# Strassen's algorithm for three weight products of a two-block transformer

## The chip, the cores and the metric

The kernel runs on one core of a Trainium2 chip. The metric is the device time in microseconds (us). The engines are TensorE (PE, the products), VectorE (DVE), ScalarE (ACT), GpSimd (POOL) and SyncE (SP, which issues the transfers from memory).

## The reference

512 tokens of 1024 features pass through two blocks of two layers each, in float32. Every layer is a mixer and then a feed-forward part, each with a normed input `h` of shape [512, 1024]:

```python
# first block, layers l = 0, 1
x = x + rms_norm(mixed @ w_out[l], attn_post_g[l])
h = rms_norm(x, ffn_pre_g[l])
y = (jax.nn.silu(h @ w_gate[l]) * (h @ w_up[l])) @ w_down[l]    # 1024 -> 2816 -> 1024
x = x + rms_norm(y, ffn_post_g[l])
# second block, layers 0 (stick-breaking attention) and 1 (a gated recurrence)
a = jax.nn.relu(h @ w1)                                         # 1024 -> 4096 -> 1024
x = x + (a * a) @ w2
```

The mixers of the first block are differential and forgetting attention. Most of the arithmetic is in the products with weights.

## The kernel before

**Numbers.** PE takes float32 in a rounded form (float32r). Each operand is kept as a high and a low part, and `mm3` (line 623) makes every product out of three: high x high, high x low, low x high. `split_into` (line 525) makes the parts: a copy (`cp`, line 313, on ACT or DVE) and a subtraction on DVE (`tt`, line 286).

**Order.** The program is first written down as a list of operations (`Program`, line 150). `schedule` (line 365) then plays it through with a cost for each operation: an engine that is free takes what is ready and due first, where `due_times` (line 335) counts back from a PE that runs without a gap in program order. A tile gets its slot when its first writer is placed; a slot is taken ahead of program order only if the rest could still run. The order found is fixed for each engine. SBUF is cut into slots by `KINDS`: 61 of 528 words ("S") for weight parts, hidden tiles and attention tiles, three raw chunks of 4.1 KB, one normed input in two parts (`xh`, `xl`), two gain rows. PSUM has four banks "A" and four "B".

**Weights.** `Stream` (line 529) loads chunks of 1024 columns (512 KB), two ahead of use, and splits each in two halves of 512.

**The feed-forward part.** `ffn` (line 1155) goes over 22 column tiles of w_gate and w_up in passes of 8, 8 and 6, `mlp` (line 1177) over 32 of w1 in four passes of 8. In a pass `proj_fm` (line 630) makes [128 features, 512 tokens] in a bank: 8 tiles of the 1024 inputs x 3 products, a weight tile of 128x128 stationary and 512 tokens moving. Then silu and the product with up (or relu and square), and the split into two parts. `proj_out` (line 667) multiplies the pass's hidden tiles by w_down or w2: hidden tiles stationary, 512 columns of weights moving.

**The entry.** The output projection ahead of a feed-forward part goes token tile by token tile (four of 128 tokens): `finish` norms the tile (`norm_tile`, line 732), and its `place` turns it on PE, four 128x128 transposes for each half of the features, and writes the parts (`cp` on ACT, the subtraction on DVE). The place of a tile comes a tile later in program order. The first four column tiles of a stage are done with `cut`: all products of tokens 0 to 255 first, then those of 256 to 511.

## Time and profile before

| what | value |
|---|---|
| median of 3 runs | 2561.39 us (2561.36 to 2562.69) |
| profiled execution, span | 2558.8 us |
| PE busy | 2524.3 us (99%) |
| DVE busy | 1591.4 us (62%) |
| ACT busy | 940.7 us (37%) |
| first feed-forward stage, with its down products | 275 to 632 us |
| second | 902 to 1258 us |
| first MLP | 1549 to 1908 us |
| second MLP | 2198 to 2559 us |

The times of the page are of one profiled execution, 2.6 us shorter than the median of the runs. An engine's busy time counts the time that its instructions last; PE's products overlap, so that the distance from one start to the next is their real price. A row of the time line gives its start, how long the group lasted, the engine, the line of the code, the operation, its tiles (output, then inputs) and shapes, and how many there are; a bracket at its end is the engine's idle time ahead of it.

### The profile page before, as it was taken

The page shows a single profiled execution, that of the slowest core. Times are in us where ns is not written, and L with a number is a line of the kernel's source. Part 1 is how long each engine was busy: PE and PEld are TensorE (multiplying, and loading weights), DVE is VectorE, ACT ScalarE, POOL GpSimd, SP SyncE. Part 2 cuts the span into 40 slices and gives each one's busy share as a digit, 9 for nine tenths or more (in the row PEclk, how much of TensorE's full clock was granted, in tenths as well). Part 3 has the DMA queues.
Part 4 walks back from the last instruction along what each step waited for, and adds up shares of the span by engine and source line. Part 5 has one row for each costly group of instructions (what it writes and reads, how often), then busy time and mean ns, then how long its engine had stood idle before and what let it go on. Part 6 is the DMA issues. An engine that isn't in the chain of part 4 may idle for free.

```text
span 2558.8 us, 36752 instructions
## 1 busy us (share of the span) xinstructions
PE 2524.3 (99%) x14060; PEld 2103.5 (82%) x14060; DVE 1591.4 (62%) x3742; ACT 940.7 (37%) x2170; POOL 57.2 (2%) x78
## 2 busy tenths in 40 slices
PE   7999999999999999999999999999999999999999
PEld 7987888888997788888898768888888887888887
DVE  8867843345886773334698887444557778744442
ACT  5656422222565532222356564222233333422210
POOL 0000000000000000000000000000000111000000
PEclk9999999999999999999999999999999999999999
DMA  6221433231322152323131114332314111342220
GB/s 204 67 83 50 137 102 99 74 116 42 109 83 67 50 181 76 97 75 115 50 100 58 42 50 149 116 99 67 106 37 129 59 59 50 118 129 76 88 77 33
DMA packets 63856, 225.12 MB, mean 88 GB/s; under 512 B 7344, under 2 KB 7984, under 8 KB 63680
## 3 DMA queue, kind: packets, MB, share of 16 engines
q1 hardware_dynamic: 63680, 222.77, 27.6%
q8 instruction: 111, 1.82, 0.3%
q14 instruction: 65, 0.53, 0.1%
HBM read 220.61 MB, written 2.13 MB: 87 GB/s over the span
## 4 chain that ended last, share of the span: by engine, by line
PE 95%; DVE 4%; issue 1%; ACT 0%; DMA 0%; SPq 0%; DVEq 0%; ACTq 0%
PE A L235 73%; PE B L235 18%; PE B L245 4%; DVE S L289 1%; DVE S L310 1%; DVE sm L304 1%; ACT S L256 0%; DVE x L304 0%; DMA gb<-in_rows_dram 0%; DVE S L317 0%; ACT xh L256 0%; DVE sm L298 0%; DVE xl L289 0%; DVE sm L297 0%; DVE S L318 0%
## 5 line engine op out<-in xcount | busy, mean ns | idle before, releaser
L235 PE MATMUL A<-xh,S 128*128 128x512 f32 (+1 forms) x3328 | 984.6, 378 | 0.0
L289 DVE TENSOR_TENSOR S<-raw,S 128x512 fp32r<-128x512 f32 (+1 forms) x792 | 523.5, 690 | 341.8 <-PE A L235 204.6
L235 PEld LDWEIGHTS A<-xh,S 128*128 128x128 f32 x3328 | 604.8, 188 | 118.0 <-issue 0.7
L235 PE MATMUL A<-xl,S 128*128 128x512 f32 (+1 forms) x1664 | 629.6, 379 | 0.0
L256 ACT ACTIVATE S<-raw 128x512 fp32r<-128x512 f32 (+1 forms) x632 | 380.9, 630 | 657.4 <-PE A L235 383.3
L235 PE MATMUL A<-S,S 128*128 128x512 f32 (+1 forms) x2088 | 511.9, 394 | 0.0
L235 PE MATMUL B<-S,S 128*128 128x512 f32 (+12 forms) x2448 | 501.2, 369 | 0.7 <-DVE S L289 0.5
L235 PEld LDWEIGHTS B<-S,S 128*128 128x128 f32 (+2 forms) x2448 | 363.2, 179 | 112.4 <-issue 31.7
L235 PEld LDWEIGHTS A<-S,S 128*128 128x128 f32 x2088 | 384.8, 188 | 83.1 <-issue 0.5
L235 PE MATMUL A<-S,xh 128*128 128x256 f32 (+1 forms) x2048 | 377.2, 286 | 0.5 <-ACT xh L256 0.2
L235 PEld LDWEIGHTS A<-xl,S 128*128 128x128 f32 x1664 | 313.0, 188 | 61.4 <-issue 0.7
L256 ACT ACTIVATE S<-A 128x512 f32<-128x512 f32 (+3 forms) x238 | 140.6, 593 | 470.0 <-PE A L235 462.4
L235 PEld LDWEIGHTS A<-S,xh 128*128 128x128 f32 x2048 | 309.3, 189 | 3.0 <-ACT xh L256 0.8
L235 PE MATMUL A<-S,xl 128*128 128x256 f32 (+1 forms) x1024 | 268.2, 285 | 1.9 <-DVE xl L289 1.9
L256 ACT ACTIVATE S<-B 128x128 f32<-128x128 f32 (+7 forms) x560 | 163.7, 360 | 110.5 <-PE B L235 64.5
L235 PEld LDWEIGHTS A<-S,xl 128*128 128x128 f32 x1024 | 183.5, 189 | 3.0 <-DVE xl L289 2.2
L289 DVE TENSOR_TENSOR S<-S,S 128x512 fp32r<-128x512 f32 (+4 forms) x234 | 133.6, 584 | 70.2 <-PE A L235 51.7
L245 PE MATMUL B<-cst,S 128*128 128x128 f32 x872 | 135.8, 276 | 27.5 <-DVE sm L298 11.5
L245 PEld LDWEIGHTS B<-cst,S 128*128 128x128 f32 x872 | 103.5, 141 | 45.2 <-DVE sm L298 11.5
L317 DVE CAST S<-raw 128x512 fp32r<-128x512 f32 (+1 forms) x160 | 68.3, 430 | 68.7 <-PE A L235 45.1
L289 DVE TENSOR_TENSOR S<-A,S 128x512 f32<-128x512 f32 (+1 forms) x68 | 46.9, 689 | 96.2 <-PE A L235 95.6
L289 DVE TENSOR_TENSOR S<-S 128x512 f32<-128x512 f32 (+2 forms) x68 | 45.5, 669 | 97.4 <-ACT S L256 55.7
(116 smaller groups left out, 1327.2 us busy)
## 6 DMA issues: line engine op xcount, KB each, us to landing
raw<-in_mlp_dram SPq DMA_DIRECT2D x128, 512.0 KB, 3.6
raw<-in_w_gate_dram SPq DMA_DIRECT2D x44, 512.0 KB, 3.6
raw<-in_w_up_dram SPq DMA_DIRECT2D x44, 512.0 KB, 3.8
raw<-in_w_down_dram SPq DMA_DIRECT2D x44, 512.0 KB, 3.7
raw<-in_w_in_tm_dram SPq DMA_DIRECT2D x28, 512.0 KB, 3.8
raw<-in_sb_qkv_dram SPq DMA_DIRECT2D x24, 512.0 KB, 4.0
raw<-in_hg_fm_dram SPq DMA_DIRECT2D x24, 512.0 KB, 3.9
raw<-in_w_in_fm_dram SPq DMA_DIRECT2D x16, 512.0 KB, 4.2
```

The costliest lines, as they stand in the source:

```text
L235: self.nc.tensor.matmul(_ap(ps), _ap(l), _ap(r), start=start, stop=stop)
L245: o = self.op([("pe", 109.0, lambda: pe.transpose(_ap(ps), _ap(src), _ap(ident)))], [src, ident], [ps])
L256: return self.nc.scalar.activation(_ap(out), _ap(src), func, **kw)
L289: alts.append(("dve", self._dve_ns(out.n), lambda: self.nc.vector.tensor_tensor(_ap(out), _ap(a), _ap(b), op)))
L304: lambda: self.nc.vector.scalar_tensor_tensor(_ap(out), _ap(a), _ap(s), _ap(b), op0, op1))],
L310: lambda: getattr(self.nc.vector, name)(_ap(out), *[_ap(v) for v in a], **kw))],
L317: return self.nc.vector.tensor_copy(_ap(out), _ap(src))
```

## The change

One level of Strassen's algorithm (in Winograd's form) for h @ [w_gate | w_up] and h @ w1. The tokens are cut in two halves, the 1024 inputs in two, and a pair of 256-column blocks of weights is the other side; seven products of half-size blocks replace eight.

- `Forms` takes the place of the normed input: seven forms of the input's blocks (a11, a12, a22, s1 to s4), each in two parts of 4 KB. Token tiles 0 and 1 give a11 and a12. Tiles 2 and 3 give s1 to s4 and a22 by four sums on DVE, and five turned tiles.
- `sched_quad` loads the four blocks of weights, makes the four sums t1, t2, t3, t4 of them on DVE, and splits seven blocks.
- `proj_quad` makes the seven products, each 24 of 256 columns (two column tiles x 4 input tiles x 3), into three banks, and adds some products up in PSUM by going on in a bank whose value was read out. Five sums out of PSUM are left to DVE, and one copy to ACT.
- Weights of all products come in slots of 4 KB (31 of kind "W", which also hold the raw chunks, the input's parts or forms, gain rows, queries, values and transposed probabilities); 30 slots of 2 KB ("S") hold the rest. Splits are of 1024 elements. Loads run up to 5 and splits up to 3 products ahead in the seven-product units.
- The square of relu may go to ACT or DVE, before it was DVE or POOL. The `cut` of a stage's first tiles is gone.

```diff
 KINDS = {
-    "S": (61, "sbuf"), "mv": (1, "sbuf"), "xh": (1, "sbuf"), "xl": (1, "sbuf"), "raw": (3, "sbuf"), "gb": (2, "sbuf"),
-    "sm": (24, "sbuf"), "rot": (4, "sbuf"), "A": (4, "psum"), "B": (4, "psum"),
+    "W": (31, "sbuf"), "S": (30, "sbuf"), "sm": (16, "sbuf"), "rot": (2, "sbuf"), "A": (4, "psum"), "B": (4, "psum"),
 }
-SLAB = 528
+SLAB = {"W": 1024, "S": 512}
...
+        def split(self, v, n):
+            w = g.tile("W", (n,), F32R), g.tile("W", (n,), F32R)
+            split_into(v, w[0].all(), w[1].all())
             return w
...
+    def sched_quad(key, blocks):
...
+        def add(out, a, b):
+            if out not in v:
+                v[out] = g.tile("W", (1024,))
+            g.tt(v[out].all(), v[a].all(), v[b].all(), ALU.add)
+
+        def make(nm, *sums):
+            def run():
+                for t in sums:
+                    add(*t)
+                return ws.split(v[nm].all(), 1024)
+            return run
...
+        plan[key] = [
+            ws.add(load(0), make(0)),
+            ws.add(load(1, 3), chain(rename("t1", 0), make("t2", ("t1", 0, 1), ("t2", "t1", 3)))),
+            ws.add(none, make("t1")),
+            ws.add(none, chain(rename("t3", 1), make("t3", ("t3", 1, 3)))),
+            ws.add(load(2), make(2)),
+            ws.add(none, make(3)),
+            ws.add(none, chain(rename("t4", "t2"), make("t4", ("t4", "t2", 2)))),
+        ]
...
+    def proj_quad(key, forms):
...
+        ids = plan[key]
+        a, c, d = PSA(), PSA(), PSA()
+
+        def product(n, bank, f, first=False):
+            wh, wl = ws.get(ids[n], (L_LOOK, F_LOOK))
+            xh, xl = forms[f]
+            for u in range(2):
+                for k in range(4):
+                    sl = slice(k * 256 + u * P, k * 256 + u * P + P)
+                    dst = bank[:, u * 256:(u + 1) * 256]
+                    one = first and not u and not k
+                    g.mm(dst, wh[:, sl], xh[:, k, :], one, False, True)
+                    g.mm(dst, wh[:, sl], xl[:, k, :], False, False, True)
+                    g.mm(dst, wl[:, sl], xh[:, k, :], False, k == 3, True)
+
+        p1, u2, u3, c12, c21, c22 = [SL() for _ in range(6)]
+        product(0, a, "a11", True)
+        g.cp(p1.all(), a.all(), only="act")
+        product(1, c, "s2", True)
+        g.tt(u2.all(), c.all(), p1.all(), ALU.add)
+        product(2, d, "s1", True)
+        product(3, c, "s3")
+        g.tt(u3.all(), c.all(), p1.all(), ALU.add)
+        g.tt(c22.all(), d.all(), u3.all(), ALU.subtract)
+        product(4, a, "a12")
+        yield 0, 0, a.all()
+        yield 1, 1, c22.all()
+        product(5, d, "s4")
+        g.tt(c12.all(), d.all(), u2.all(), ALU.subtract)
+        yield 1, 0, c12.all()
+        product(6, c, "a22")
+        g.tt(c21.all(), c.all(), p1.all(), ALU.add)
+        yield 0, 1, c21.all()
...
+    class Forms:
...
+        def put(self, f, h, t):
+            w = self.xs[f]
+            put_parts(w[0][:, 0:4, tok(t % 2)], w[1][:, 0:4, tok(t % 2)], turned(h))
+
+        def finish(self, t, gain):
+            hs = norm_tile(t, gain)
+            if t >= 2:
+                (a11, a12), (a21, a22) = self.held.pop(t - 2), hs
+                s1, s2 = SL(), SL()
+                g.tt(s1.all(), a21.all(), a22.all(), ALU.subtract)
+                g.tt(s2.all(), s1.all(), a11.all(), ALU.subtract)
+                g.tt(a21.all(), a11.all(), a21.all(), ALU.subtract)
+                g.tt(a12.all(), a12.all(), s2.all(), ALU.add)
+
+            def place():
+                if self.xs is None:
+                    self.xs = new_forms()
+                if t < 2:
+                    self.put("a11", hs[0], t)
+                    self.put("a12", hs[1], t)
+                    self.held[t] = hs
+                else:
+                    for f, h in (("s2", s2), ("s1", s1), ("s3", a21), ("s4", a12), ("a22", a22)):
+                        self.put(f, h, t)
...
     def ffn(l, xs, pre, nxt):
         def up(lo, hi):
-            parts = []
+            blocks = []
             for j in range(lo, hi, 2):
...
+                for n, t, v in proj_quad(("gu", l, j), xs):
+                    if n == 0:
+                        gate[t] = SL()
+                        g.a(gate[t].all(), v, AF.Silu)
+                    else:
+                        out[t] = v
+                for t in range(2):
+                    g.tt(gate[t].all(), out[t], gate[t].all(), ALU.mult)
+                blocks.append([hidden(gate[t].all()) for t in range(2)])
```

## Rows read from the trace of the kernel before

**Rows 1.** Page, busy time of each engine with its share of the span.

```profile
PE 2524.3 (99%) x14060; PEld 2103.5 (82%) x14060; DVE 1591.4 (62%) x3742; ACT 940.7 (37%) x2170; POOL 57.2 (2%) x78
```

**Rows 2.** Waits of PE: total us, times, longest (ten rows).

```profile
PE B L245 <- DVE sm L298: 11.5, 1, 11.5
PE B L245 <- DVE S L317: 8.1, 6, 1.7
...
PE A L235 <- DVE xl L289: 1.9, 1, 1.9
...
PE A L235 <- DVE S L289: 0.2, 1, 0.2
```

**Rows 3.** Chain that ended last: shares, then pieces (start, us, what).

```profile
PE 95%; DVE 4%; issue 1%; ACT 0%; DMA 0%; SPq 0%; DVEq 0%; ACTq 0%
...
27.12 29.31 PE A L235 x248
...
365.54 22.21 PE B L235 x96
387.76 111.12 PE A L235 x480
...
2198.69 4.49 PE A L235 x38
```

**Rows 4.** Groups by line and form: count, busy us and mean ns, idle before.

```profile
L235 PE MATMUL A<-xh,S 128*128 128x512 f32 x2816 | 893.1, 396 | 0.0
L235 PEld LDWEIGHTS A<-xh,S 128*128 128x128 f32 x3328 | 604.8, 188 | 118.0 <-issue 0.7
L235 PE MATMUL A<-xl,S 128*128 128x512 f32 x1408 | 557.8, 397 | 0.0
...
L235 PE MATMUL A<-xh,S 128*128 128x256 f32 x512 | 92.1, 282 | 0.0
...
L235 PE MATMUL A<-xl,S 128*128 128x256 f32 x256 | 71.8, 280 | 0.0
```

**Rows 5.** Time line of PE at the entry of the first feed-forward stage.

```profile
266.83 7.74 PE L235 MATMUL A<-S,S 128*128 128x512 f32 x33
274.42 1.03 PE L245 MATMUL B<-cst,S 128*128 128x128 f32 x8
275.21 0.36 PE L235 MATMUL A<-xh,S 128*128 128x256 f32 x1
...
284.87 1.03 PE L245 MATMUL B<-cst,S 128*128 128x128 f32 x8
```

**Rows 6.** Time line of PE at the entry of the first MLP.

```profile
1548.16 1.04 PE L245 MATMUL B<-cst,S 128*128 128x128 f32 x8
...
1553.48 1.03 PE L245 MATMUL B<-cst,S 128*128 128x128 f32 x8
```

**Rows 7.** Rates of DVE and ACT: time line rows, then groups by form.

```profile
287.35 2.49 DVE L289 TENSOR_TENSOR S<-raw,S 128x512 fp32r<-128x512 f32 x4
...
1550.38 2.71 ACT L256 ACTIVATE S<-raw 128x512 fp32r<-128x512 f32 x5
...
L317 DVE CAST S<-raw 128x512 fp32r<-128x512 f32 x156 | 66.5, 430 | 65.6 <-PE A L235 45.1 <-DMA raw<-in_mlp_dram 5.2 <-PE B L235 4.9
...
L289 DVE TENSOR_TENSOR S<-S,S 128x511 f32<-128x511 f32 x16 | 10.3, 684 | 0.0
...
L289 DVE TENSOR_TENSOR S<-S,S 128x383 f32<-128x383 f32 x16 | 8.9, 554 | 0.9
```

**Rows 8.** Stretch: its length, busy of PE, PEld, DVE, ACT, POOL; clock, DMA, GB/s.

```profile
286.00:308.00 22.00, 22.00 (x151) 20.30 (x150) 18.75 (x34) 7.65 (x14) 0.00 (x0) 1.00 0.63 206
```

**Rows 9.** The start: stretch with its granted clock, then time line rows.

```profile
18.00:20.50 2.50, 2.35 (x13) 2.29 (x13) 2.50 (x14) 1.77 (x3) 0.00 (x0) 1.00 0.46 125
...
18.80 0.63 PE L235 MATMUL A<-S,xh 128*128 128x256 f32 x2
19.23 0.41 PE L235 MATMUL A<-S,xl 128*128 128x256 f32 x1
```

More of the change, by code (lines that the diff above doesn't have):

```diff
@@ L552, in ahead, with __init__ @@
-        def ahead(self, i):
-            while self.n < len(self.todo) and self.n <= i:
-                self.emit(self.n)
-                self.n += 1
-        def get(self, ids):
-            w = []
-            for i in ids:
-                self.ahead(i + self.look)
-                w += self.done.pop(i)
-            return w
-    ws = Stream(W_LOOK)
-    plan = {}
-    def sched(key, a, width=1024):
-        plan[key] = [ws.add(a[:, c:min(c + width, a.shape[-1])]) for c in range(0, a.shape[-1], width)]
+        def __init__(self):
+            self.todo, self.done = [], {}
+            self.loaded = self.made = 0
@@ new lines, in add, with ahead @@
+        def add(self, load, make):
+            self.todo.append((load, make))
+            return len(self.todo) - 1
+        def split(self, v, n):
+            w = g.tile("W", (n,), F32R), g.tile("W", (n,), F32R)
+            split_into(v, w[0].all(), w[1].all())
+            return w
+        def ahead(self, i, looks=(W_LOOK, W_LOOK)):
+            for what, look in ((0, looks[0]), (1, looks[1])):
+                at = self.made if what else self.loaded
+                while at < len(self.todo) and at <= i + look:
+                    if what:
+                        self.done[at] = self.todo[at][1]()
+                    else:
+                        self.todo[at][0]()
+                    at += 1
+                if what:
+                    self.made = at
+                else:
+                    self.loaded = at
@@ new lines, in get, with raw_load, sched @@
+        def get(self, i, looks=(W_LOOK, W_LOOK)):
+            self.ahead(i, looks)
+            return self.done.pop(i)
+    def raw_load(src):
+        n = src.shape[-1]
+        v = g.tile("W", (n,))
+        g.dma(v.all(), src, nbytes=P * n * 4)
+        return v
+    ws = Stream()
+    plan = {}
+    def sched(key, a, n):
+        k, per = a.shape[-1] // n, 1024 // n
+        ids = []
+        for c in range(0, k, per):
+            src, box = a[:, c * n:min(c + per, k) * n], []
+            ids.append(ws.add(lambda src=src, box=box: box.append(raw_load(src)),
+                              lambda box=box: ws.split(box[0].all(), box[0].dims[0])))
+        plan[key] = (ids, per, n, k)
@@ L651, in proj_tm, with x_part, proj_fm, tokens_by @@
+    def x_part(xs, k, sl):
+        return tuple(w[:, k % 2, sl] for w in xs[k // 2])
+    def proj_fm(key, xs):
+        part, ps = weights(key), PSA()
+        for k in range(KT):
+            mm3(ps.all(), part(k), x_part(xs, k, slice(0, S)), k == 0, k == KT - 1)
+        return ps
+    def tokens_by(ps, t, part, xs):
+        for k in range(KT):
+            mm3(ps, x_part(xs, k, tok(t)), part(k), k == 0, k == KT - 1)
     def proj_tm(key, xs):
-        slabs = ws.get(plan[key])
+        part = weights(key)
@@ L667, in proj_out @@
     def proj_out(key, parts, evac, finish=None, banks=(PSA, PSA)):
+        kn = plan[key + (0,)][3]
         if finish:
-            slabs, rest = [ws.get(plan[key + (c,)]) for c in range(2)], []
+            part, rest = [weights(key + (c,)) for c in range(2)], []
             for t in range(NT):
@@ L756, in norm_tile, with turned, put_parts @@
-        return place
+        return hs
+    def turned(h):
+        tr = PSB()
+        for k in range(4):
+            g.tr(tr[:, tok(k)], h[:, tok(k)], ident)
+        return tr.all().rearrange("p (k t) -> p k t", k=4)
+    def put_parts(dst, lo, src):
+        g.cp(dst, src, only="act")
+        g.tt(lo, src, dst.bitcast(F32), ALU.subtract)
     def END(t):
         return lambda: None
-    class Next:
+    class Plain:
         xs = None
-        def placing(self, place):
-            def run():
+        def finish(self, t, gain):
+            hs = norm_tile(t, gain)
+            def place():
@@ L931, in attn_pair @@
     def attn_pair(vtile, probs):
-        pts = [[SL() for _ in range(NT)] for _ in range(2)]
+        two = [g.tile("W", (2, S)) for _ in range(NT)]
+        pts = [[w[:, hh, :] for w in two] for hh in range(2)]
         ready = {}
```

287 lines of the change are left out of this document (152 added, 135 removed).

## The prediction

> **What bounds the kernel now.** I read the page's busy table first [rows 1]: TensorE (PE) is busy 99% of the 2558.8 us span, VectorE (DVE) 62%, ScalarE (ACT) 37%. A pipelined PE can look busy without being at its rate, so I then read the list of all that PE waited for [rows 2]: ten rows, 30.8 us in all, of which 13.4 us belong to the start (the first row and the xl row). Some 17 us are left in 2545 us. The chain that ended last says the same: PE holds 95% of it [rows 3], and in the feed-forward stages it is one unbroken run of products. So a microsecond of PE work that goes is a microsecond of span, until another engine or a wait is late.
>
> Two pitches carry the sum, both start to start. A product of 512 columns: 480 of them in 111.12 us, 96 in 22.21 us, so 231.4 ns [rows 3]. A product of 256 columns against a 128x128 stationary tile: 248 in 29.31 us in the projections, 38 in 4.49 us in the token-half group of an MLP, so 118.2 ns [rows 3]; the latter has the very operand form (weights stationary, 256 tokens moving) that the change uses everywhere. Half the columns cost 51%. A single weight load lasts 188 ns [rows 4], and loads and products overlap: neither pitch holds a whole one.
>
> **The products.** Take as a unit two gate and two up column tiles (FFN) or four w1 tiles (MLP): 38 units, 11 in each FFN and 8 in each MLP. The groups by form confirm the count: 2816+1408 products of 512 columns with x moving, less 960 of other projections, are 34 units of 96, and 512+256 of 256 columns are 4 units done by token halves (192 each) [rows 4]. A unit is 96 x 231.4 ns = 22.21 us now. Seven half-size products are 7 x 24 = 168 of 256 columns, 168 x 118.2 ns = 19.86 us. Gain 2.35 us x 38 = 89.5 us; the four halved units cost 192 x 118.2 = 22.69 us each now, 0.48 us more, so 1.9 us go too: **-91.4 us**.
>
> What could undo this is the weight load that comes with each product, 168 a unit in place of 96. In the token-half group a load and its product, on full 128-row tiles, take 118.2 ns together [rows 3, 4]. The Trainium skill, "TensorE: Matmul & The Clock Gate", section "The mechanism" (Part 3), says otherwise: that a weight load overlaps running products only where it goes to other rows of the array. By that rule a unit would take at least 168 x 188 ns = 31.6 us; the trace disagrees, and I take the row (the rule's case is rival d).
>
> **More transposes.** Token tiles 2 and 3 now turn five half-width forms each (20 transposes) instead of two (8): 24 more at each of four entries to a feed-forward stage. Eight go by in 0.79 us (274.42 to 275.21) [rows 5]: 96 x 0.099 = **+9.5 us**, on PE and not hidden.
>
> **The entry to each stage.** Now, when the last output product of token tile 3 ends, PE does the first unit on token tiles 0 and 1 while tile 3 is normed. At the first FFN that lasts from 275.21 to the transposes of tile 3 at 284.87, 10.5 us after the products ended at about 274.4; at an MLP, with one norm instead of two, from 1548.1 to 1553.48, 5.3 us [rows 5, 6]. The cover was up to 96 products, 11.3 us. After the change only the a11 product and, if its weights are ready, the a12 product need no token of tile 3: 24 x 0.1182 = 2.84 us each, with 2.0 us for the transposes of tile 2. The chain grows too: two DVE sums until s2 (2 x 0.60), three more low parts of tile 2 on the busy DVE (1.8), then transpose, ACT copy, low part (0.4 + 0.2 + 0.6 + 0.7) and hand-overs of some 0.4. That puts the s2 product at 10.5 + 5.3 = 15.8 us (FFN) or 5.3 + 5.3 = 10.6 us (MLP) after the last output product, against a cover of 4.8 to 7.7 us. Idle: 8.1 to 11.0 us at an FFN, 2.9 to 5.8 us at an MLP. Some of the chain is slack (two weight splits lie in it), so I take 8.5 and 4: 2 x 12.5 = **+25 us**, bounds 16 and 34.
>
> **DVE and ACT in the units.** This is where it can fail. A 512-element DVE add or subtract repeats every 0.60 us (four in 2.49 us) and lasts 1.02 ns per element more (511 against 383 elements: 684 and 554 ns) [rows 7], so one of 1024 is 0.60 + 0.53 = 1.13 us. A unit now needs 8 low parts of weights, 4.8 us. After: 7 low parts and 4 sums of 1024 (12.5 us), five sums out of PSUM (3.0), four more for the hidden tiles (2.4): 17.9 us per 19.86 us of PE, 90% of it. ACT: a 512 copy repeats every 0.52 us (five in 2.71) [rows 7], so one of 1024 takes 1.04 us at most: 7 x 1.04 + 0.5 + 2.1 = 9.9 us (FFN), 14.0 us (MLP, with squares). DVE just fits, and PE waits only where a bank is handed over late. The tightest: the a12 product (2.84 us) runs while DVE must form u3 and then c22 before the s4 product may add to bank d. That is 0.2 + 0.60 + 0.69 + 0.2 = 1.7 us, and up to 1.13 us more if a weight split has just begun: 2.83 us against 2.84. One split more between the two costs 1.1 us. I take 0.15 us per unit, **+6 us**; bounds 0 (nothing below: the product rate is measured) and 1.0 us per unit, 38 us. In the first 22 us of the first FFN DVE was already busy 18.75 us [rows 8], and PE had no idle there. The down products follow each few units at a third of that load, so a lag is caught up only as far as buffers allow.
>
> DMA carries the same weights: four loads of 512 KB per unit, some 106 GB/s, against 206 GB/s seen in that stretch [rows 8]. On SP's queue a load that waits for one of the 31 W slots holds up the gain rows and the weights behind it; the splits ahead wait for those. Stretches with 14 slots held by the seven forms are the place to look.
>
> **Everything else.** Attention and the recurrent mixer keep their products, with 4 KB and 2 KB slots (31 and 30) in place of 61 small ones and tiles of their own. A start split is 0.53 us longer per part. No row shows what the new partition costs; the nearest is the 17 us of PE waits left in the span [rows 2], which could vanish or double: -17 to +17, and I take **+4 us** since long splits get in the way of short chains.
>
> **Sum.** -91.4 + 9.5 + 25 + 6 + 4 = -46.9 us. The profiled span of 2558.8 us would be 2511.9; the median of the runs is 2.6 us above that span, so **2514.5 us**.
>
> **Rivals.** (a) The entries are well covered and DVE is in time: 16 for entries, 0 for hand-overs, -5 for the rest: 2561.4 - 91.4 + 9.5 + 16 - 5 = 2490.5 us. For it: the planner does work as soon as it is due. Chance 0.17.
>
> (b) PE loses its clock at the entries. At the start, after 11.5 us of nothing, 256-column products came 0.21 us apart until 20.6 us and 0.118 us from then on, though the granted clock reads 1.00 throughout [rows 9]; gaps of up to 1.77 us later changed no pitch [rows 2]. The Trainium skill, "TensorE: Matmul & The Clock Gate", section "The HAM clock gate", says that an idle PE falls to half of 2.4 GHz and needs activity to be released, which agrees with the pitch and not with the printed clock. With some 24 slow products per entry, 24 x 0.09 x 4 = 9 us, and dearer entries (34): 2533 us. Chance 0.18.
>
> (c) Slower: the hand-overs of PSUM. Outside the units the change costs 9.5 + 25 + 4 = 38.5 us against 91.4 gained, so 52.9 us remain, 1.39 us per unit. If DVE is late by more than that at each unit (two splits in the way at c22, or DVE needing over 21.2 us per unit because copies are planned onto it as well: a 512 copy lasts 0.43 us there [rows 7], so five or six of 1024 would do), it is slower. At 1.7 us per unit: 2561.4 - 52.9 + 65 = 2573 us. For it: DVE at 90% with in-order queues; against it: splits are made three products ahead. Chance 0.11.
>
> (d) The weight loads stop hiding: 168 x 0.188 = 31.6 us per unit, 9.4 us dearer, 38 x 9.4 = 357 us, 2957 us with the other terms. Both pitches refute it: 0.01.
>
> **How the numbers follow.** My forecast (2500 to 2530) has 0.49, (a) 0.17, (b) 0.18, (c) 0.11, (d) 0.01; 0.04 lies between (b) and no gain. The range 2489 to 2548 takes in (a) in most of its width, and (b), and leaves out (c), (d) and the tails of the bounds: about 0.8. About 0.2% (5 us) is what a measurement here can tell from no change: faster 0.85, same 0.04, slower 0.11.
>
> **What would show it.** Right: 168 products per unit at 118 ns, 38 x 168 of them; DVE busy up by some 400 us; PE waits at four entries of 4 to 9 us on the s2 parts; few waits inside units. Wrong: a list of PE waits on DVE in every unit, above all ahead of the fourth, sixth and seventh product; a pitch near 0.19 or 0.21 us; waits on weights still loading; or PE waits in attention of much over 20 us.

## The result and the profile after

| | before | after | forecast |
|---|---|---|---|
| median of the runs | 2561.38 us (4 runs) | 2523.25 us (4 runs, 2521.36 to 2524.82) | 2514.5 us (2489 to 2548) |
| ratio | 1 | 0.985 (95% interval 0.9836 to 0.9864) | |
| profiled span | 2558.8 us | 2523.0 us | 2511.9 us |

The change is worth 38 us, where 47 were forecast. The direction was right and the time lies in the range, but the stages show that several terms of the sum were off and made up for each other in part.

The first view is the page of the kernel after: busy time of each engine, its share of the span, its instructions. It answers to [rows 1].

```profile
PE 2463.5 (98%) x16508; PEld 2192.8 (87%) x16508; DVE 1938.0 (77%) x3726; ACT 1099.8 (44%) x2150; POOL 59.1 (2%) x78
```

PE is still the bound. DVE has 347 us more work (400 were expected) and stays at 77%. The second view is the list of PE's waits (total us, times, longest), to be held against [rows 2]:

```profile
PE B L246 <- ACT S L257: 15.3, 4, 7.4
PE B L246 <- DVE sm L299: 11.9, 2, 11.1
PE B L246 <- DVE S L290: 11.4, 11, 1.8
PE B L246 <- DVE sm L310: 3.5, 1, 3.5
PE B L246 <- DVE S L324: 3.4, 2, 3.3
PE A L236 <- ACT S L257: 3.3, 3, 1.5
...
PE A L236 <- DVE W L290: 1.3, 2, 0.7
PE A L236 <- DVE S L290: 0.8, 1, 0.8
```

L246 is a transpose, L236 a product. The 11.1 us belong to the start, as the 11.5 us did before. New are the four waits of a transpose on `S` from ACT (15.3 us): two of over 7 us, at the entries to the two feed-forward stages of the first block. The 3.5 and 3.3 us stand at the start of two mixers. Products of bank A, those of the units, wait for some 2 us on DVE in all: the hand-overs of banks are in time.

The third view is the chain that ended last, with the lines of the first MLP (start, us, what), against [rows 3]:

```profile
1552.87 36.96 PE A L236 x308
1589.83 21.79 PE B L236 x96
1611.62 62.07 PE A L236 x432
```

308 products of 256 columns in 36.96 us are 120.0 ns each; 96 down products of 512 in 21.79 us are 227.0 ns. The last row holds both kinds: 96 x 0.227 and 336 x 0.120 us, two units.

The fourth view is the time line of PE at the entry of the first feed-forward stage, against [rows 5], and, behind the dots, of the first MLP, against [rows 6]:

```profile
270.48 8.42 PE L236 MATMUL A<-W,S 128*128 128x512 f32 x36
278.74 0.60 PE L246 MATMUL B<-cst,S 128*128 128x128 f32 x4
279.10 0.72 PE L236 MATMUL A<-W,W 128*128 128x256 f32 x4
...
284.34 0.50 PE L236 MATMUL A<-W,W 128*128 128x256 f32 x2
292.11 1.11 PE L246 MATMUL B<-cst,S 128*128 128x128 f32 x4 [7.27 <-ACT S L257]
293.70 2.60 PE L246 MATMUL B<-cst,S 128*128 128x128 f32 x12 [0.48 <-DVE S L290]
...
296.06 0.66 PE L236 MATMUL A<-W,W 128*128 128x256 f32 x2
...
374.26 2.91 PE L236 MATMUL B<-W,S 128*128 128x512 f32 x12
...
1541.22 1.91 PE L246 MATMUL B<-cst,S 128*128 128x128 f32 x16
...
1547.94 0.50 PE L236 MATMUL A<-W,W 128*128 128x256 f32 x2 [1.52 <-ACT S L257]
1548.60 3.60 PE L246 MATMUL B<-cst,S 128*128 128x128 f32 x16
1551.85 0.59 PE L236 MATMUL A<-W,W 128*128 128x256 f32 x2
...
1589.67 2.68 PE L236 MATMUL B<-W,S 128*128 128x512 f32 x11
```

After the last output product (278.74) only the a11 product and two more run (in the kernel's order the first two of the a12 product, which need only the high part of its weights); from 284.84 PE is idle for 7.27 us, until the normed tile 3 is there. At the MLP the gap is 1.52 us, and something else ends it: the two products of bank A at 1547.94 wait for ACT's copy out of that bank (ACT, 1547.31, 0.58 us). Tile 3 is normed there at 1548.45. The next products behind the transposes of tile 3 start 17.3 us after the last output product at the feed-forward stage (296.06) and 10.6 us after it at the MLP (1551.85). The last transposes of the entry are slow: 16 of them from 1548.60 to the next product at 1551.85 are 203 ns each, while the 16 from 1541.22 to 1542.89 took 104 ns each.

These starts give the account of the feed-forward stages. From 278.74 to the first down product at 374.26 are 95.5 us, of which four units of 168 x 0.120 = 20.16 us are 80.6: the entry costs 14.9 us. Before it is, from 274.42 [rows 5] to the first down product at 365.38 (its piece of the chain begins 0.16 us later, [rows 3]), 91.0 us less four units of 22.21: 2.1 us. The same sum over all stages:

| us | before | after | change | forecast |
|---|---|---|---|---|
| 38 units | 38 x 22.21 = 844.0 | 38 x 20.16 = 766.1 | -77.9 | -89.5 |
| four entries (transposes, idle time, halved first units) | 2.1, 2.4, 2.0, 2.1 | 14.9, 15.2, 8.1, 8.3 | +37.9 | +32.6 |
| 2592 down products | 231.4 ns | 227 ns | -11.4 | 0 |
| hand-overs in units, ends of stages (what is left) | | | +0.6 | +6 |
| the four mixers | 274.4, 255.8, 276.3, 290.1 | 278.7, 262.0, 281.8, 289.0 | +15.0 | +4 |
| sum | 2558.8 | 2523.0 | -35.8 | -46.9 |

(The forecast's entry is its 9.5 + 25 less the 1.9 of the halved units. By the medians the change is -38.1: the profiled execution is the slowest of the four.)

### The profile page after: what moved, and what is told of

Its sections match the earlier page's. It is cut to its first block, busy times and chain, and to the rows that moved or that the text cites. A ratio compares the mean times of both kernels' runs of the same rounds, so it can differ in the third digit from the quotient of the medians.

```text
span 2523.0 us, 41492 instructions
## 1 busy us (share of the span) xinstructions
PE 2463.5 (98%) x16508; PEld 2192.8 (87%) x16508; DVE 1938.0 (77%) x3726; ACT 1099.8 (44%) x2150; POOL 59.1 (2%) x78
## 3 DMA queue, kind: packets, MB, share of 16 engines
q1 hardware_dynamic: 63968, 222.77, 26.9%
## 4 chain that ended last, share of the span: by engine, by line
PE 45%; DVE 4%; issue 1%; ACT 1%; POOL 0%; POOLq 0%; DVEq 0%
PE A L236 33%; PE B L236 10%; PE B L246 2%; DVE S L316 1%; DVE S L290 1%; DVE W L290 1%; DVE sm L310 0%; ACT W L257 0%; ACT S L257 0%; DVE S L324 0%; DVE x L310 0%; POOL S L292 0%; DVE W L323 0%; POOL sm L292 0%; DVE sm L299 0%
## 5 line engine op out<-in xcount | busy, mean ns | idle before, releaser
L236 PE MATMUL A<-W,W 128*128 128x256 f32 (+2 forms) x10416 | 1444.5, 296 | 5.5 <-ACT S L257 3.3
L236 PEld LDWEIGHTS A<-W,W 128*128 128x128 f32 x10416 | 1327.3, 192 | 47.0 <-ACT S L257 3.9
L290 DVE TENSOR_TENSOR W<-W,W 128x1024 fp32r<-128x1024 f32 (+1 forms) x664 | 804.4, 1220 | 264.1 <-PE A L236 186.8
L257 ACT ACTIVATE W<-W 128x1024 fp32r<-128x1024 f32 (+1 forms) x425 | 444.5, 1056 | 669.1 <-PE A L236 387.0
L236 PE MATMUL A<-W,S 128*128 128x512 f32 (+1 forms) x2088 | 501.8, 390 | 0.0
L236 PEld LDWEIGHTS A<-W,S 128*128 128x128 f32 x2088 | 384.4, 188 | 76.1 <-issue 0.9
L236 PE MATMUL B<-W,S 128*128 128x512 f32 (+2 forms) x1952 | 368.9, 347 | 0.2
L236 PEld LDWEIGHTS B<-W,S 128*128 128x128 f32 (+1 forms) x1952 | 294.6, 178 | 59.6 <-issue 6.1
L257 ACT ACTIVATE S<-S 128x512 f32<-128x512 f32 (+4 forms) x275 | 165.9, 620 | 91.1 <-DVE S L290 71.2
L290 DVE TENSOR_TENSOR S<-S,S 128x512 fp32r<-128x512 f32 (+7 forms) x316 | 185.1, 606 | 17.7 <-ACT S L257 9.0
L246 PE MATMUL B<-cst,S 128*128 128x128 f32 x840 | 140.5, 294 | 48.5 <-ACT S L257 15.3
L246 PEld LDWEIGHTS B<-cst,S 128*128 128x128 f32 x840 | 105.9, 150 | 71.0 <-ACT S L257 17.2
L257 ACT ACTIVATE S<-B 128x128 bf16<-128x128 f32 (+7 forms) x280 | 105.1, 422 | 124.0 <-PE B L236 88.1
L257 ACT ACTIVATE S<-A 128x512 f32<-128x512 f32 (+2 forms) x139 | 82.1, 591 | 143.5 <-PE A L236 138.4
L257 ACT ACTIVATE W<-B 128x128 f32<-128x128 f32 (+3 forms) x373 | 107.8, 362 | 58.7 <-PE B L246 57.2
L236 PE MATMUL B<-S,W 64*128 64x256 f32 (+5 forms) x384 | 94.9, 387 | 1.9 <-DVE W L323 1.4
L257 ACT ACTIVATE W<-A 128x512 f32<-128x512 f32 (+2 forms) x76 | 42.7, 581 | 86.2 <-PE A L236 77.7
L236 PEld LDWEIGHTS B<-S,W 64*128 64x128 f32 (+1 forms) x384 | 52.1, 186 | 29.7 <-issue 17.5
L257 ACT ACTIVATE S<-S,sm 128x512 f32<-128x512 f32 (+3 forms) x85 | 50.4, 595 | 56.9 <-DVE sm L310 35.3
```

The source lines that it names most:

```text
L236: self.nc.tensor.matmul(_ap(ps), _ap(l), _ap(r), start=start, stop=stop, skip_group_check=shared)
L246: o = self.op([("pe", 109.0, lambda: pe.transpose(_ap(ps), _ap(src), _ap(ident)))], [src, ident], [ps])
L257: return self.nc.scalar.activation(_ap(out), _ap(src), func, **kw)
L290: alts.append(("dve", self._dve_ns(out.n), lambda: self.nc.vector.tensor_tensor(_ap(out), _ap(a), _ap(b), op)))
```

## Experiments

Five questions were open. What is the saving of Strassen's algorithm itself, beside that of the new slots and long splits that came with it? Why is the pitch now 227 and 120 ns, and so regular? What does the entry cost, and can it be covered? Is DVE near its limit in the units? What do the mixers lose? All times below are medians against the same kernel before, with the 95% interval of the ratio where it carries a verdict.

### The layout alone

The kernel after, with eight plain products in each unit (the normed input in two parts, no forms); its slots, splits of 1024 and loads are kept.

```diff
-        plan[key] = [
-            ws.add(load(0), make(0)),
...
+        plan[key] = [ws.add(load(n), make(n)) for n in (0, 2, 1, 3)]
...
+        halves = ((0, 256), (256, 512)) if key[2] == 0 else ((0, 512),)
+        for c0, c1 in halves:
+            for w in range(2):
+                for u in range(2):
...
+                            mm3(pss[w, u][:, c0:c1], (wh[:, sl], wl[:, sl]), x_part(xs, 4 * i + k, slice(c0, c1)),
+                                not i and not k, bool(i and k == 3))
```

> The changed kernel with the seven products taken back: w_gate, w_up and w1 are multiplied by the eight plain products of 512 columns (the first group of a stage by token halves), with the plain normed input; the 4 KB and 2 KB slots, the splits of 1024, the load order and everything in the mixers stay as changed. So it is the new layout alone. My theory: the mixers are about 15 us slower because of the layout (they were +4.3, +6.3, +5.5, -1.1 us in the changed kernel), while all products of 512 columns come every 227 ns in place of 231.4, which gives the feed-forward stages 38 x 0.42 + 12 = 28 us: 2561 + 15 - 28 = 2548 us. Rival: the mixers lose because of the forms and sums next to them, and the layout costs them nothing: 2533 us, with mixers as before. Second rival: the pitch of 227 ns belongs to the short products beside it, not to the layout: 2576 us.

2550.37 us, ratio 0.9958 (0.9944 to 0.9973). Its chain, in the first feed-forward stage:

```profile
368.64 21.76 PE B L236 x96
390.40 108.80 PE A L236 x480
```

The pitch of 512 columns is 226.7 ns without Strassen's algorithm: it belongs to the layout. So do the mixers' losses: 278.3, 262.6, 283.3 and 287.9 us, +15.6 in sum against +15.0 in the kernel after. Strassen's algorithm itself is worth 2550.4 - 2523.3 = 27.1 us. That closes by parts: a unit goes from 21.76 to 20.16 us (-1.60 x 38 = -60.8), the entries from 12.6 to 46.5 us (+33.9): -26.9.

### The kernel before, with slots 2048 bytes apart

Why did the layout change the pitch? Before, a slot of kind S was 528 words, so that two slots lie 2112 bytes apart; after, 2048 or 4096. Here the kernel before gets slots of 512 words, and eight more of 528 for what doesn't fit; to make room, chunks are loaded one ahead into two raw slots. Nothing else is changed.

```diff
-W_LOOK = 2
+W_LOOK = 1
...
-    "S": (61, "sbuf"), "mv": (1, "sbuf"), "xh": (1, "sbuf"), "xl": (1, "sbuf"), "raw": (3, "sbuf"), "gb": (2, "sbuf"),
+    "S": (56, "sbuf"), "V": (8, "sbuf"), "mv": (1, "sbuf"), "xh": (1, "sbuf"), "xl": (1, "sbuf"), "raw": (2, "sbuf"), "gb": (2, "sbuf"),
...
+                kind = "S" if n // 2 <= S else "V"
+                w = g.tile(kind, (n // 2,), F32R), g.tile(kind, (n // 2,), F32R)
```

> The kernel before, with its small slots 2048 bytes apart (56 of them) in place of 2112; the one chunk with slabs of 528 words has eight slots of its own, and to make room weights are loaded one chunk ahead in place of two, with two raw chunks in place of three. A shift of all slots by 64 bytes left the changed kernel's pitch at 227 and 120 ns, so the absolute start is not it; what the kernel before has alone is slots that start at all different distances from each other's 2048-byte steps. Theory: with slots in step the 512-column products come every 227 ns and the 256-column ones every 120, here too, and the 4300 products give 19 us: about 2543 us, if one chunk ahead is enough to feed PE (if not, more, but the pitch in the rows tells). Rival: the pitch goes with something else (the size of a split, the tiles that hold x): 231 and 118 ns as before, 2561 us.

2533.45 us, ratio 0.9892 (0.9877 to 0.9907), 27.7 us less than before. Its chain, where [rows 3] have 22.21 and 111.12 us for the same products of 512 columns, and 29.31 us for 248 of 256 columns:

```profile
27.04 29.27 PE A L235 x244
...
364.31 21.76 PE B L235 x96
386.07 108.80 PE A L235 x480
```

226.7 ns, in every one of them; the 256 columns take 120.0 ns here too, in place of 118.2. That loads go one chunk ahead can't be the cause: the kernel after loads two ahead, as the kernel before does, and has the same pitch. The gain is 10 us more than I expected. My 4300 products were too few: the feed-forward stages alone have 34 x 96 + 2592 = 5856 of 512 columns, and at 4.7 ns each that is 27.5 us. The mixers stay at the times of before (273.7, 255.6, 276.8, 288.4 us). So most of what the change as a whole gained is to be had without it: over this kernel it is worth 10.2 us.

### All slots moved by 64 bytes

Is it the slots' distance from each other, or where the first one begins? A tile of 16 words ahead of all pools of the kernel after moves every slot.

```diff
     pools = {}
+    ahead = ctx.enter_context(tc.tile_pool(name="ahead", bufs=1))
+    ahead.tile([P, 16], F32, tag="ahead", name="ahead")
```

> The changed kernel with 64 bytes left free ahead of its slots, so that every weight, form and hidden tile starts 64 bytes further on in its partition; nothing else differs. In the kernel before slots were 2112 bytes (33 x 64) apart, and its products of 512 columns came every 226 to 237 ns (231.4 in the mean), those of 256 every 113 to 122 (118.2); in the changed one, with slots at multiples of 2048, it is 227 and 120 throughout. Theory: the pitch goes by where operands start, so here the 512-column pitch is spread again around 231 and the 256-column one around 118: some 4300 x 4.4 = +19 us and 10400 x -1.8 = -19 us, 2523 us in all, but with both pitches changed in the rows. Rival: the start address does not matter (the chunk sizes or the mix of products do): 227 and 120 as now, 2523 us.

2524.24 us (0.9855, 0.984 to 0.9869), the same as after, with the same 227 and 120 ns (96 products in 21.79 us, 308 in 36.95). A common shift by 64 bytes does not matter. Slots 2112 bytes apart also begin at many different places between two multiples of 2048, and this run tried only one other, so it does not part distance from start altogether.

### The a12 product second

In the first unit of each stage, the a12 product (tokens 0 to 255 alone) runs second in place of fifth, and its block is loaded and split second.

```diff
+        if key[2] == 0:
+            p0 = ws.add(load(0), make(0))
+            p4 = ws.add(load(2), make(2))
...
         g.cp(p1.all(), a.all(), only="act")
+        if key[2] == 0:
+            product(4, a, "a12")
+            yield 0, 0, a.all()
         product(1, c, "s2", True)
```

> The changed kernel, with the a12 product and its weights put second in the first unit of each of the four stages (in the other units it stays fifth). My theory: in the changed kernel only the a11 product ran in an entry, since the block for a12 was loaded and split fifth; 2.9 us more cover at each entry, less about 1 us where the sixth product now waits for c22 with nothing in between: 4 x 1.9 = 7.6 us, 2515.5 us. Rival: its weights are split by the same DVE that the norm chain needs, so the chain ends later by as much: 2523 us.

2518.21 us, ratio 0.9831 (0.9816 to 0.9846): 5.0 us less than after. The time line of PE at the first entry:

```profile
283.22 3.13 PE L236 MATMUL A<-W,W 128*128 128x256 f32 x24 [1.10 <-ACT S L257]
290.02 0.65 PE L246 MATMUL B<-cst,S 128*128 128x128 f32 x4 [3.67 <-ACT S L257]
```

The cover that I had reckoned with is there now, and the wait is 3.7 in place of 7.3 us. The four entries cost 13.9, 12.9, 6.9 and 6.9 us, 40.6 in place of 46.5. The gain is smaller than a product of 24 (2.9 us) at each of them, since at the first the product itself waits for 1.10 us, and at an MLP there were only 1.52 us to cover. There the wait is now 0.75 us, and the granted clock stays at 1.00.

### Forms in the order of their use

Tile 2's forms are held back and turned pair by pair with those of tile 3 (s2 of both first), in order that DVE has less to do ahead of tile 3's norm.

```diff
+                elif t == 2:
+                    self.held[t] = (s2, s1, a21, a12, a22)
                 else:
-                    for f, h in (("s2", s2), ("s1", s1), ("s3", a21), ("s4", a12), ("a22", a22)):
-                        self.put(f, h, t)
+                    other = self.held.pop(2)
+                    for n, (f, h) in enumerate((("s2", s2), ("s1", s1), ("s3", a21), ("s4", a12), ("a22", a22))):
+                        self.put(f, other[n], 2)
+                        self.put(f, h, 3)
```

> The changed kernel, with the forms of token tile 2 turned together with those of tile 3, form by form (s2 of tile 2, s2 of tile 3, s1 of tile 2, ...), so that DVE's low parts of tile 2 stand behind tile 3's norm chain and not in it. My theory: at an FFN entry, tile 3's chain of small DVE steps took 6.3 us (280.1 to 286.5) where 2.1 us was its own length, because nine 512-element operations of tile 2 lay between its steps; without them PE's idle of 7.3 us falls to about 4 and the MLP entries gain half a microsecond: 2523 - 7 = 2516 us. Rival: DVE has the same work to do before the s2 product either way, and the turns of tile 2 now come late as well: 2523 us or a little more.

2524.09 us (0.9854): no gain. The entries cost 15.1, 17.7, 6.5 and 6.5 us. My theory fell: the planner takes what is ready, so program order alone does not keep tile 2's work out of tile 3's chain. At the first entry the work only moved. Tile 3's first norm (of the output) takes 2.5 us up to the update of x (279.49 to 282.01), but four sums and three low parts now stand in its second norm (of x), which takes from 284.54 to 290.49; in the kernel after it goes from 289.17 to 291.34.

### The chain ahead of all else

In the planner an engine that has something ready waits up to 250 ns for another operation, if that one is due earlier by URGENT. Here that margin is 1000 ns in place of 8000, together with the two edits above.

```diff
-URGENT = 8000.0
+URGENT = 1000.0
```

> The kernel with the a12 product second, the forms turned form by form, and a planner that lets an engine wait a moment (250 ns) for an operation that is due 1 us earlier than what is ready, in place of 8 us. Form by form alone changed nothing (2524.1 us): DVE still took 680 ns operations of token tile 2 into the 60 ns gaps between the small steps of tile 3's norm chain, since they were ready. Theory: the length of that chain sets the entry; with it unbroken (2.1 us in place of 4 to 6 at an FFN entry) PE's idle there falls by 3 to 4 us at each FFN and 1 at each MLP: 2518 - 8 = 2510 us. Rival: the work pushed back is needed for the same s2 product, and waiting engines lose elsewhere: 2518 us or more.

2546.64 us, ratio 0.9943 (0.9927 to 0.996): 23 us more than after, where 13 less were expected. PE's waits:

```profile
PE B L246 <- ACT S L257: 17.9, 2, 8.9
PE B L246 <- DVE S L324: 16.3, 8, 11.1
PE A L236 <- DVE W L290: 14.2, 5, 6.0
```

The wait at the two entries grew to 8.9 us, and at the start of two mixers products wait for low parts (5.8 and 6.0 us, at 658.63 and 1287.40). The entries cost 53.3 us, the mixers 1125.4 in place of 1111.6 us. An engine that holds still for one chain loses more in the others.

### Tile 2 without DVE

How much of an entry is DVE's work on tile 2? On the version with halved splits (below), tile 2's sums are left out, and its five forms are made of the normed halves by two copies on ACT each, with no low parts. The products and transposes are all there.

```diff
-            if t >= 2:
+            if t == 3:
...
+                    if t == 2:
+                        for f, h in (("s2", hs[0]), ("s1", hs[0]), ("s3", hs[0]), ("s4", hs[1]), ("a22", hs[1])):
+                            w, tr = self.xs[f], turned(h)
+                            for part in w:
+                                g.cp(part[:, 0:4, tok(0)], tr, only="act")
```

> The kernel with halved splits and the a12 product second (2512.8 us), and at the four entries token tile 2's forms without DVE: its four sums are left out (the normed halves stand in for the forms), and both parts of each form are copied by ACT, so the low parts of tile 2 are not made. That takes 9 x 0.60 = 5.4 us of DVE work from each entry and adds five ACT copies. It tests what PE's idle at the entry goes by. Theory: DVE's whole work between the last output product and the s2 product (it is busy without a gap there), so the s2 product comes 3 to 5 us earlier at an FFN and 1.5 to 3 at an MLP: 9 to 16 us less, 2497 to 2504 us. Rival: the latency of tile 3's own chain of dependent steps, which the order of the rest does not touch (turning form by form changed nothing): 2 us less at most, 2511 us.

2505.95 us, ratio 0.9782 (0.9768 to 0.9797): 6.9 us less than the version it is made from, 9.5 less in the profiled spans. That lies between my theory (2497 to 2504 us) and the rival (2511). DVE's time line at the first entry of the kernel after shows what is taken away:

```profile
280.13 0.15 DVE L290 TENSOR_TENSOR sm<-sm 128x1 f32<-128x1 f32 x1
280.19 0.68 DVE L290 TENSOR_TENSOR S<-A,W 128x512 f32<-128x512 f32 x1
280.79 0.14 DVE L299 TENSOR_SCALAR sm<-sm 128x1 f32<-128x1 f32 x1
280.85 0.68 DVE L290 TENSOR_TENSOR S<-S,S 128x512 f32<-128x512 f32 x1
281.45 0.15 DVE L298 TENSOR_SCALAR sm<-sm 128x1 int32<-128x1 int32 x1
281.52 0.68 DVE L290 TENSOR_TENSOR S<-S,S 128x512 f32<-128x512 f32 x1
...
283.72 0.68 DVE L290 TENSOR_TENSOR W<-B,W 128x512 fp32r<-128x512 f32 x1
...
286.64 1.41 DVE L310 SCALAR_TENSOR_TENSOR x<-S,sm,x 128x512 f32<-128x512 f32 x2
```

and that of this kernel, with the same steps of the norm:

```profile
278.61 0.15 DVE L290 TENSOR_TENSOR sm<-sm 128x1 f32<-128x1 f32 x1
278.79 0.15 DVE L299 TENSOR_SCALAR sm<-sm 128x1 f32<-128x1 f32 x1
...
279.42 1.31 DVE L310 SCALAR_TENSOR_TENSOR sm<-sm,sm 128x1 f32<-128x1 f32 x6
280.76 1.41 DVE L310 SCALAR_TENSOR_TENSOR x<-S,sm,x 128x512 f32<-128x512 f32 x2
```

From the first small step of tile 3's norm to the update of x are 6.5 us in the one (280.13 to 286.64) and 2.15 in the other (278.61 to 280.76): eight operations of tile 2 (three sums, five low parts) at 0.6 us or more apart stood between steps of 0.15 us. The version that this kernel is made from lies between them (278.11 to 283.58, 5.5 us). The kernel before took 2.24 us for the same steps:

```profile
276.42 0.15 DVE L289 TENSOR_TENSOR sm<-sm 128x1 f32<-128x1 f32 x1
...
278.66 1.42 DVE L304 SCALAR_TENSOR_TENSOR x<-S,sm,x 128x512 f32<-128x512 f32 x2
```

The entries come to 9.8, 10.9, 5.1 and 5.1 us, 30.8 in place of 41.0. A part remains at the first-block stages, since products of bank A then wait for ACT's copies (`PE A L236 <- ACT S L257`, 5.7 us in two).

### Tile 2's sums on GpSimd

The same relief without leaving anything out: the four sums of tile 2 may go to POOL.

```diff
-                g.tt(s1.all(), a21.all(), a22.all(), ALU.subtract)
+                g.tt(s1.all(), a21.all(), a22.all(), ALU.subtract, pool="any" if t == 2 else False)
...
```

> The kernel with halved splits and the a12 product second (2512.8 us), in which the four sums of token tile 2's forms may go to POOL (1.5 us each there, 0.60 on DVE) where the planner finds that earlier. Theory: DVE's work sets the entry; with 2.4 us of it gone from each FFN entry, and less at the MLPs, PE starts the s2 product some 1.5 to 2 us earlier there: 2512.8 - 5 = 2508 us. Rival: the sums were done in gaps, and POOL's are slower than the chain that they stand in: 2513 to 2516 us.

2513.04 us against 2512.84 of the version it is made from: nothing, with the entries at 41.1 us. The time line of POOL and then of DVE at the first entry:

```profile
274.92 3.82 POOL L292 TENSOR_TENSOR S<-S,S 128x512 f32<-128x512 f32 x2 [257.45 <-ACT S L257]
...
278.78 0.69 DVE L290 TENSOR_TENSOR S<-S,S 128x512 f32<-128x512 f32 x1 [1.18 <-POOL S L292]
279.39 0.15 DVE L290 TENSOR_TENSOR sm<-sm 128x1 f32<-128x1 f32 x1
...
284.12 1.42 DVE L310 SCALAR_TENSOR_TENSOR x<-S,sm,x 128x512 f32<-128x512 f32 x2
```

POOL took two of the sums, at 1.9 us each, DVE waited 1.18 us for them, and the five low parts still stand in the norm. It takes 4.7 us (279.39 to 284.12) in place of 5.5, but begins 1.3 us later.

### The entry filled with products

While PE would wait, it does products of a11 that nobody reads (64 at the first block's stages, 24 at an MLP), so as to see what the clock costs.

```diff
+        if key[2] == 0:
+            idle = PSB()
+            xh = forms["a11"][0]
+            for i in range(64 if key[0] == "gu" else 24):
+                g.mm(idle[:, 0:256], xh[:, i % 4, 0:P], xh[:, i % 4, :], True, True)
```

> The changed kernel, with products of 256 columns that nothing uses (of the a11 form with itself, into a spare bank) in the first unit of each stage: 64 at an FFN entry (7.7 us), 24 at an MLP entry (2.9 us), due after the s2 product, so that PE takes them while it has nothing else. It takes no work away. My theory: the half clock that the changed kernel shows at each entry comes from the idle time; with it filled the granted clock stays at 1.00 there, and the 15 or so transposes at each entry come every 109 ns in place of 213: 4 x 1.6 = 6.5 us less, and 1 to 2 us more for products left over: 2518 us. Rival: the clock falls for another reason (transposes do not count, or the start of a stage does it), and the fill only costs: 2524 to 2528 us, clock as now.

2522.84 us (0.9847, 0.983 to 0.9863): no difference from after that can be told. The views are busy times in a stretch (length, PE, PEld, DVE, ACT, POOL, granted clock, DMA share, GB/s). Of the kernel after, the second row at an entry, the third at the start of a mixer, the fourth at an MLP:

```profile
282.00:289.00 7.00, 2.70 (x21) 2.16 (x19) 6.96 (x19) 3.77 (x8) 0.00 (x0) 1.00 0.10 38
289.10:295.90 6.80, 3.31 (x15) 2.92 (x16) 6.42 (x19) 2.14 (x4) 0.00 (x0) 0.50 0.00 0
651.00:654.40 3.40, 3.33 (x16) 3.36 (x17) 2.51 (x9) 2.19 (x7) 0.00 (x0) 0.50 0.00 0
1548.70:1552.10 3.40, 3.40 (x17) 3.34 (x18) 3.15 (x6) 1.80 (x3) 0.00 (x0) 0.50 0.00 0
```

and of the filled one:

```profile
289.10:295.90 6.80, 5.93 (x45) 4.97 (x45) 6.66 (x12) 3.72 (x6) 0.00 (x0) 1.00 0.00 0
```

In the kernel after, the clock falls to the lower of its two levels (0.50 of 2.4 GHz) at each of the four entries; filled, it stays at the upper one. But the entries went only from 46.5 to 44.6 us. The slow transposes cost 1.6 us each time by their rows, and some 0.5 us on the path: at the higher clock PE waits for DVE's low parts instead. The fill itself costs up to 0.3 us at the first entry, where tile 3 is normed at 290.30 and its transposes start at 290.60. A mixer of that run was 3.0 us longer, with a stretch at half clock that the kernel after hasn't; so the median says nothing either way, and this experiment decides only that the clock isn't the main cost.

### More work for DVE in the units

Rival (c) had DVE at its limit from five or six more copies per unit. Here three of the four weight sums of a unit (t2, t3, t4) are each followed by a product with a column of ones, about 3.4 us of DVE per unit by the forecast's rates.

```diff
+                for _ in range(1 if sums else 0):
+                    g.tt(v[nm].all(), v[nm].all(), one_col.to_broadcast([P, 1024]), ALU.mult)
```

> The changed kernel with DVE work added: the sums t2, t3 and t4 of each unit's weights are each multiplied by one once more before they are split (three operations of 1024 elements per unit, 3 x 1.13 = 3.4 us; values stay the same). This tests how near the units are to DVE's limit: 17.9 us of DVE work per unit become 21.3, against 20.16 us of PE (168 x 120 ns). Theory (DVE has 2.3 us of room per unit, and can work ahead by a few products only): the units become DVE's, 1.1 us each, less what the down products let it catch up: 15 to 44 us more, 2538 to 2567 us. Rival (the room is much larger, since DVE works ahead through the down products): under 5 us more, 2528 us. Rival (hand-overs of banks were already in time by a hair, and now miss at each unit): over 60 us more.

2524.69 us, 1.4 us more than after, within both kernels' scatter. The page's busy line:

```profile
PE 2462.4 (98%) x16508; PEld 2189.3 (87%) x16508; DVE 2027.5 (80%) x3784; ACT 1146.9 (45%) x2206; POOL 58.9 (2%) x78
```

DVE takes 89 us more work and ACT 47: the planner moved copies from the one to the other, and the down products after each few units leave room to work ahead. The units do not stall.

### Halved splits in the mixers

On the version with the a12 product second, weights of the plain products (projections, output, down) are split by two copies and two subtractions of 512, as before the change, into the new slots.

```diff
+        def split_halves(self, t, n):
+            w = g.tile("W", (n,), F32R), g.tile("W", (n,), F32R)
+            for c0, c1 in ((0, n // 2), (n // 2, n)):
+                split_into(t[:, c0:c1], w[0][:, c0:c1], w[1][:, c0:c1])
+            return w
...
-                              lambda box=box: ws.split(box[0].all(), box[0].dims[0])))
+                              lambda box=box: ws.split_halves(box[0], box[0].dims[0])))
```

> The kernel with the a12 product second (2518.2 us), and on top of it the weights of all other products (mixers, down products) split in halves of 512 elements in their 4 KB slots, as the kernel before did, while those of the seven-product units stay at 1024. It tests what in the layout costs the mixers 15 us. Theory: long splits (1.13 us on DVE, in order) get in the way of short chains, as at the two entries into plain mixers where PE idles 3.3 to 3.5 us against 1.7 before: 5 to 8 us less, 2511 us. Rival: it is the number and size of slots (30 for hidden and attention tiles, 31 for the rest), which stays: 2518 us, or 2520 with some 200 more short DVE and ACT instructions.

2512.84 us, ratio 0.9809 (0.9794 to 0.9823), 5.4 us less than the version without. The mixers take 275.6, 261.2, 279.7 and 288.8 us, in sum 4.9 us less (1105.4 for 1110.3). At the start of two of them PE waits for 2.80 and 2.65 us in place of 3.44 and 3.28, and the granted clock stays at 1.00 there. It is the fastest version that leaves nothing out, 48.5 us below the kernel before and 10.4 below the kernel after.

## Why the prediction was right, and where its sum was off

**The mechanism held.** Products were the bound, a unit has 168 of half the columns in place of 96, and a weight load for each stays hidden. The Trainium skill, "TensorE: Matmul & The Clock Gate", section "The mechanism" (Part 3), has loads overlap only with products on other rows of the array; here the trace disagrees again, on full tiles: 308 pairs at 120.0 ns, with loads that last 192 ns in the mean (10416 of `A<-W,W`). Rival (d) is out. (The prediction's remark that neither pitch holds a whole load of 188 ns is true of 118.2 ns alone.)

That the sum came within 11.1 us of the measured change is in part luck. By the table the units were 11.6 us dearer than forecast, the entries 5.3 and the mixers 11.0, the down products 11.4 us cheaper and the hand-overs 5.4.

**Products: -91.4 was too much.** The counts were right, both pitches were not those of the new kernel. 256 columns take 120.0 ns, not the 118.2 of [rows 3] (+11.4 us over 38 units). And 231.4 ns for 512 columns was no property of the product, but of slots 2112 bytes apart, as the experiment on the kernel before shows: 226.7 with 2048. In that layout Strassen's algorithm saves 1.60 us a unit, 61 us, not 2.35 us and 89. Of the 77.9 us that the units gained against the kernel before, 17 are the slots' (0.45 us a unit). The same layout took 11.4 us off the down products, a term that the sum did not have; by chance it cancelled the dearer 256 columns.

**Transposes, +9.5:** 96 more at 104 ns (1541.22 to 1542.89) are 10.0 us. Right.

**Entries, +25: the right mechanism, too cheap.** With the transposes and less the halved units 32.6 us were forecast and 37.9 came; the term by itself is 37.9 - 10.0 + 1.9 = 29.8 us. The idle time itself (7.27 and 7.4 us at the first block's stages, 1.52 at each MLP) is below my 8.5 and 4, but the a12 product did not cover: its weights were not split in time. Products that need tile 3 start 17.3 and 10.6 us after the last output product, where I had 15.8 and 10.6: right at the MLP, too early at the first block's stages. The step that failed there is the order on DVE. I charged 1.8 us for three more low parts of tile 2, and did not see that three of its sums and all five low parts would stand between the small steps of tile 3's norm: that stretch takes 6.5 us, in the kernel before 2.24. Without tile 2's work on DVE the entries cost 10.2 us less: 1.8 us at each MLP, as much as I charged, but 4.1 and 2.4 us at the first block's stages.

**Rival (b), the clock, was half right.** The granted clock does read 0.50 at all four entries, after PE's idle time. The Trainium skill, "TensorE: Matmul & The Clock Gate", section "The HAM clock gate", says that of an idle PE, and here the trace agrees. My reading of [rows 9], that the printed clock might not show it, is not borne out at these places. The 1.00 of [rows 9] tells nothing: the trace of the kernel before has no record of the clock ahead of 20.13 us, and the view prints 1.00 from 0 to 11 us too, where PE had done nothing yet. Its price was not 9 us: 1.6 us at an entry by the transposes' rows, and some 0.5 us of span when the filled entry took it away.

**Hand-overs, +6, and rival (c).** At most 2 us of waits inside units, and DVE bears 89 us more work in all. The 90% that I worked out for DVE were right for a unit by itself, but they are no limit: copies go to ACT, and splits are made ahead during the down products. A slower result by that way was further off than 0.11 says. Rival (a) had this term right, at 0, and its other two wrong (16 for entries that measured 29.8, -5 for the rest that measured +15.0).

**The rest, +4, was the worst term:** +15.0 in the mixers, near the bound of 17. It comes with the layout, not with the algorithm (+15.6 with eight plain products). The long splits account for about 5 us. At the start of two mixers PE waits for 3.5 and 3.3 us in place of up to 1.77 before, and then has a stretch at half clock (651.0 above). With halved splits those waits are shorter and that stretch is gone, so some of this is in the 5 us already. The first mixer has such a stretch too (0.50 from 19.5 to 26.3 us); what these stretches cost was not tried. Some 9 us are left with halved splits (1105.4 against 1096.6 us). What the division into 31 and 30 slots costs by itself stays open.

## What to carry to other kernels

An algorithm that trades products for sums is paid at the places where the sums cannot be hidden: here 61 us of PE time were saved and 34 were lost again at four entries, some 10 of them because the new sums and low parts stood on the engine that also carries the serial chain. Before you price a saving by a measured pitch, look whether the pitch is regular and the same elsewhere in the kernel; and measure the new layout with the old algorithm, or you credit the one with what the other did. List an engine's real order at the entry, small steps included, rather than adding the new operations at the end.

## What the runs showed of the hardware

How the SBUF slots of the operands lie changes the rate of TensorE. With slots 2112 bytes apart, 512 columns of float32r against a 128x128 tile come every 231.4 ns; with 2048 or 4096 bytes every 226.7 to 227.0 ns. A shift of all slots by 64 bytes changes nothing. For 256 columns the same step goes the other way, 118.2 to 120.0 ns. In the kernel before it was worth 27.7 us in all, 1.1%, together with the shorter look-ahead that made room for it. What in the chip makes the difference no run here tells.

A wait of 1.52 us at an entry (up to 1547.94) went with a fall of the granted clock to 0.50 at 1548.70, while waits of up to 1.77 us in the kernel before went with none that the profile records.
